# One engine for the low parts of the weights, and new durations in the planner that sets the order

## Chip, core and metric

One core of one Trainium2 chip. The metric is the device time of one execution in microseconds, the median of several runs. The profile is one execution taken by the hardware profiler.

## What is computed

Two layers over 256 tokens of width 1024 (cut to what matters):

```python
for l in range(DEPTH):                       # DEPTH = 2
    proj = x @ w_in[l]                       # split into the branches' inputs and the gates
    ya = rg_lru(conv(pa_x), ...) * gelu(pa_g)               # branch A
    yb = rms(gated_delta_rule(q, k, v, g, beta)) * silu(z)  # branch B
    yc = rms(gla(q, k, v, log_a)) * silu(r)                 # branch C
    merged = sum(sigmoid(gate_i) * (y_i @ w_branch[l, i]) for y_i in (ya, yb, yc))
    x = layer_norm(alpha * x + merged @ w_out[l])
    x = layer_norm(alpha * x + (silu(x @ w1[l]) * (x @ w3[l])) @ w2[l])
```

All in float32. Branch B solves, for each chunk of tokens and each head, a unit triangular system; the kernel does this by inverting 8x8 blocks first and joining them step by step.

## The kernel before

**Weights.** All weight matrices of a layer are cut into 146 units of 128x1024 float32 in the order in which TensorE uses them (`ORDER`, `NU`). SyncE's queue loads each unit into one of four `raw` tiles (`load_w`). `split_w` then makes two tiles of it in a rounded format that TensorE takes at full rate: ScalarE copies `raw` to `hi`, and the low part `lo = raw - hi` is a tensor_tensor of 128x1024 elements. Each matmul of the reference becomes three: x_hi with hi, x_lo with hi, x_hi with lo. Most `lo` are made by VectorE (line 304); of the units with an even number from 8 to 58 of each layer, 26 a layer, GpSimd makes them (line 432). These units belong to the first part of a layer, the projections and branches. `fill` keeps 6 split units ahead of TensorE (14 in the last branch). After each split the next unit's load is issued.

**Main work and chains.** `main` is a generator that emits TensorE's units in the order of `ORDER`: `tm` and `fm` (projections), `br`, `wo`, `f` and `w` (the feed-forward part). Everything that follows from a product (convolutions, activations, the triangular solve with its small matmuls `pk`, `pR`, `px`, `pp`, `pt`, the norms) sits in other generators, the chains, each with a priority. A chain yields at each point where it has to wait for something.

**The planner.** Each engine runs its instructions in the order in which they are emitted, so the emission order decides how a late result holds up an engine. `Order` works it out while the program is built: it keeps a clock for each engine, `op` adds a cost to it for each instruction (formulas in the helpers: `act_fn`, `dve`, `mm`, `tp` and so on), and `drive` emits a chain's next step when, by these clocks, its inputs were ready `SLACK` = 1.5 us before TensorE's clock (priority 0: no slack) and neither ScalarE's nor VectorE's clock is more than `LOAD` = 9 us ahead of TensorE's. Otherwise it emits the next piece of main work. Real waits are made by semaphores; a cost that is wrong moves an instruction in its engine's order, nothing else. A step put too early makes TensorE wait in place; one put too late delays its chain.

**Branch B's chain** (`b_inv`), as far as the text needs it: ScalarE scales the products `pk` into `At`; VectorE multiplies `At` with the decay `E`; a copy of 128x64 elements starts `z` (inside the tile `sub`); a product `pR` follows; then a loop of 14 small dependent VectorE instructions alternates between `pR` and `z`; one VectorE instruction spreads `z` into `Y`; and TensorE transposes `Y` (`px`). After it come the joining steps `pp`, `pt`, `px`. GpSimd also computes the inverse square roots (`rsqrt`: `rk`, `rq`, `ycf`, `ybf`, `rs`), of 8 columns or of one.

Of the kernel before, what the change touches and what calls it, by code (L numbers as in the profile page):

```python
# [8 lines left out]
F32 = mybir.dt.float32  # L9
# [6 lines left out]
MULT, ADD, SUB, MAX, MIN = ALU.mult, ALU.add, ALU.subtract, ALU.max, ALU.min  # L16
# [7 lines left out]
NF = FF // P  # L24
ALPHA = float((2.0 * L) ** 0.25)
RAW, AHEAD, FAR, SLACK, SLOTS = 4, 6, 14, 1.5, 37
PMOD, PLO, PHI = 2, 8, 60
LOAD = (99.0, 9.0, 9.0, 9.0, 9.0)
DKB = float(128 ** -0.5)
DKC = 0.125  # L30
# [42 lines left out]
NU = len(ORDER)  # L73
# [81 lines left out]
          AF.Silu: "u", AF.Gelu_apprx_tanh: "g"}  # L155


class Order:


# [12 lines left out]
    def op(self, eng, cost, ready=0.0):  # L173
        t = max([self.clk[eng], self.ready, ready] +
                [f for e, f in self.fin.items() if e != eng])
        t += cost
        self.clk[eng] = t
        self.fin[eng] = t
        return t

    def end(self):
# [68 lines left out]
def _build(ctx, nc, tc, ins, out):  # L250
    V, A, G, T = nc.vector, nc.scalar, nc.gpsimd, nc.tensor
    pool = lambda name, bufs, **k: ctx.enter_context(tc.tile_pool(name=name, bufs=bufs, **k))
# [6 lines left out]
    O = Order()  # L259
    def TOK(i):  # L260
        tc.stamp_issue_order_token(i.ins, "tbl")
    def PIN(i):
        if MODE == 2: TOK(i)
        else: tc.keep_in_program_order(i)
    def n_of(ap):
        n = 1
        for d in ap.shape[1:]:
            n *= d
        return n

    def slot(name, dt=F32):
        return t4.tile([P, 1024], dt, tag="t4k", name=name)
# [11 lines left out]
    def act_fn(o, i, f, **k):  # L284
        aps = sum(not isinstance(v, float) for v in k.values())
        sets = TABLES.get(f)
        if sets is not None and O.table not in sets:
            O.table = sets[0]
            O.op("act", 1.28)
            if f == AF.Exp:  # L290
                PIN(A.preload_act_table_set("natural_log_exp_and_others"))
        ins_ = A.activation(o, i, f, **k)  # L292
        if sets is not None and MODE:
            TOK(ins_)
        O.op("act", 0.12 + 0.09 * aps + 0.000833 * n_of(o))

    def cp(o, i):
        act_fn(o, i, AF.Copy)

    def dve(o, x=0.0):  # L300
        O.op("dve", 0.13 + x + 0.00104 * n_of(o))

    def tt(o, a, b, op):
        V.tensor_tensor(out=o, in0=a, in1=b, op=op)  # L304
        dve(o)
# [8 lines left out]
    def stt(o, a, s, b, op0, op1):  # L314
        V.scalar_tensor_tensor(out=o, in0=a, scalar=s, in1=b, op0=op0, op1=op1)  # L315
        dve(o, 0.06)
# [16 lines left out]

    def recip(o, i):
        V.reciprocal(o, i)
        dve(o, 0.0075 * n_of(o))

    def rsqrt(o, i, e):
        G.tensor_tensor(out=o, in0=i, in1=e, op=ALU.pow)  # L339
        O.op("pool", 0.3 + 0.17 * n_of(o))  # L340

    def split(hi, lo, src):
        cp(hi, src)
        tt(lo, src, hi.bitcast(F32), SUB)

    def mm(o, w, x, start=True, stop=True):
        T.matmul(o, w, x, start=start, stop=stop)  # L347
        n, m = n_of(x), n_of(w)
        if w.dtype == F32R:
            O.op("pe", max(n, m, 128) / 2400.0)  # L350
        else:
            O.op("pe", max(n, m, 32) / 600.0)

    def tp(o, i, idn):
        T.transpose(o, i, idn)  # L355
        O.op("pe", 0.107)

    def h4(t):
        return t.rearrange("p (h c) -> p h c", h=4)
# [37 lines left out]
    raws, ready, pos = [], [], [0, 0]  # L397

    def halves(i):
        n = 512 if i < 1 else 1024  # L400
        return [slice(c, c + n) for c in range(0, 1024, n)]

    def load_w(between=None):
        i = len(raws) + pos[1]
        if i >= L * NU:
            return
        l, j = divmod(i, NU)
        t = wraw.tile([P, 1024], F32, tag="raw", name="raw")
        for c in halves(i):
            nc.sync.dma_start(out=t[:, c], in_=ins["w"][l, j][:, c])  # L410
            if i == 0 and c.start == 0:
                between()
        O.clk["dma"] = max(O.clk["dma"], O.clk["pe"] - 4.0) + 1.5
        raws.append((t, O.clk["dma"] + 2.0))

    def split_w(between=None):
        if not raws:
            return
        t, at = raws.pop(0)
        i, j = pos[1], pos[1] % NU  # L420
        pos[1] += 1
        keep = O.ready, O.fin
        O.begin(at)
        hi, lo = slot("hi", F32R), slot("lo", F32R)
        for c in halves(i)[:-1]:
            split(hi[:, c], lo[:, c], t[:, c])
            between()
        c = halves(i)[-1]
        hi_, lo_, t_ = hi[:, c], lo[:, c], t[:, c]
        cp(hi_, t_)  # L430
        if j % PMOD == 0 and PLO <= j < PHI:
            G.tensor_tensor(out=lo, in0=t, in1=hi.bitcast(F32), op=SUB)  # L432
            O.op("pool", 2.4)
        else:
            tt(lo_, t_, hi_.bitcast(F32), SUB)
        ready.append((hi, lo, O.end()))
        O.ready, O.fin = keep
        load_w()
# [61 lines left out]
    def layer(l, xs, xtok):  # L500
# [5 lines left out]
        def done(n):  # L506
            O.done(k_(n))
# [527 lines left out]
        def ln_chain(tk, halves, lv, xs_out, is_out, name):  # L1035
            g, b = lv
            s = xr[:, tk]
            c = 512 if len(halves) == 2 else 256
            st = sml.tile([P, 4, 6], F32, tag="st", name="st")
            c0 = 0  # L1040
            for n, ps in enumerate(halves):
                sl = slice(c0, c0 + ps.shape[1])
                yield k_(f"{name}ps{tk}{n}")
                stt(s[:, sl], s[:, sl], ALPHA, ps, MULT, ADD)
                if tk and n:
                    yield
                for c0 in range(sl.start, sl.stop, c):
                    V.bn_stats(st[:, c0 // c], s[:, c0:c0 + c])
                    O.op("dve", 0.1 + 0.001 * c)
                c0 = sl.stop  # L1050
            mv, rs = sm("mv", [P, 2]), sm("rs", [P, 1])
            V.bn_aggr(mv, st[:, 0:D // c].rearrange("p a b -> p (a b)"))
            ts(rs, mv[:, 1:2], 1e-5, ADD)
            rsqrt(rs, rs, mhalf[:, 0:1])
            if is_out and tk:
                dst = out[tk * P:(tk + 1) * P]
                c, nb = slice(768, 1024), sm("nb", [P, 1])
                stt(nb, mv[:, 0:1], -1.0, rs, MULT, MULT)
                act_fn(s[:, c], s[:, c], AF.Identity, scale=rs, bias=nb)
                G.tensor_tensor(out=s[:, c], in0=s[:, c], in1=g[:, c], op=MULT)  # L1060
                G.tensor_tensor(out=s[:, c], in0=s[:, c], in1=b[:, c], op=ADD)
                A.dma_start(out=dst[:, c], in_=s[:, c])
                for c in (slice(0, 384), slice(384, 768)):
                    stt(s[:, c], s[:, c], mv[:, 0:1], g[:, c], SUB, MULT)
                    stt(s[:, c], s[:, c], rs, b[:, c], MULT, ADD)
                    nc.sync.dma_start(out=dst[:, c], in_=s[:, c])
                return
            h = [slice(0, 512), slice(512, 1024)]
            stt(s[:, h[0]], s[:, h[0]], mv[:, 0:1], g[:, h[0]], SUB, MULT)
            stt(s[:, h[0]], s[:, h[0]], rs, b[:, h[0]], MULT, ADD)  # L1070

            def second():
                stt(s[:, h[1]], s[:, h[1]], mv[:, 0:1], g[:, h[1]], SUB, MULT)
                stt(s[:, h[1]], s[:, h[1]], rs, b[:, h[1]], MULT, ADD)

            def fm(n, between):
                ps = h4(bank("pln"))
                for q in range(4):
                    c0 = 512 * n + 128 * q
                    tp(ps[:, q], s[:, c0:c0 + P], ident)  # L1080
                o = [[xs_out[i][2 * n + q][:, :, tk * P:(tk + 1) * P] for q in range(2)]
                     for i in range(2)]
                for q in range(2):
                    cp(o[0][q], ps[:, 2 * q:2 * q + 2])
                between()
                for q in range(2):
                    tt(o[1][q], ps[:, 2 * q:2 * q + 2], o[0][q].bitcast(F32), SUB)

            if is_out:
                nc.sync.dma_start(out=out[tk * P:(tk + 1) * P, h[0]], in_=s[:, h[0]])  # L1090
                second()
                nc.sync.dma_start(out=out[tk * P:(tk + 1) * P, h[1]], in_=s[:, h[1]])
                return
            yield
            fm(0, second)
            yield
            fm(1, lambda: None)
            done(f"{name}{tk}")
            if tk:
                ahead[0] = AHEAD  # L1100
# [250 lines left out]
    with tc.manual_schedule(engines={mybir.EngineType.SP}):  # L1351
# [9 lines left out]
        for q in range(4):  # L1361
            if q % 2 == 0:
                tp2 = pair2("xin")
            t = tp2[q % 2]
            n = 1 if q else 2
# [99 lines left out]
```

## Time and profile before

| | us |
|---|---|
| median of 3 runs | 942.83 (942.8, 942.83, 944.91) |
| profiled execution | 939.84 |
| its span, first to last instruction | 938.0 |

The profiled execution is 1.84 us longer than its span. Busy times in the profile are per engine; a matmul's end is modelled, and consecutive matmuls overlap, so that TensorE's rate is read from the starts of consecutive matmuls and not from their lengths. "PE" is TensorE, "DVE" VectorE, "ACT" ScalarE, "POOL" GpSimd, "SPq" SyncE's queue.

### The profile page before, as it was taken

The page shows a single profiled execution, that of the slowest core. Times are in us where ns is not written, and L with a number is a line of the kernel's source. Part 1 is how long each engine was busy: PE and PEld are TensorE (multiplying, and loading weights), DVE is VectorE, ACT ScalarE, POOL GpSimd, SP SyncE. Part 2 cuts the span into 40 slices and gives each one's busy share as a digit, 9 for nine tenths or more (in the row PEclk, how much of TensorE's full clock was granted, in tenths as well). Part 3 has the DMA queues.
Part 4 walks back from the last instruction along what each step waited for, and adds up shares of the span by engine and source line. Part 5 has one row for each costly group of instructions (what it writes and reads, how often), then busy time and mean ns, then how long its engine had stood idle before and what let it go on. Part 6 is the DMA issues. An engine that isn't in the chain of part 4 may idle for free.

```text
span 938.0 us, 15814 instructions
## 1 busy us (share of the span) xinstructions
PE 922.5 (98%) x6306; PEld 838.3 (89%) x6306; DVE 644.5 (69%) x965; ACT 523.6 (56%) x824; POOL 162.4 (17%) x81
## 2 busy tenths in 40 slices
PE   7999999999999999999999999999999999999996
PEld 5998899999988888888889998999999888888885
DVE  5577975695875776676457699586768648667715
ACT  5877669644733665555145774973547147566600
POOL 0454512530000000000033351253300000000001
PEclk9999999999999999999999999999999999999998
DMA  8854324546770865568325352255568338655801
GB/s 273 266 182 148 101 69 130 173 149 234 249 290 3 299 215 180 182 240 275 111 72 191 121 158 96 72 155 195 181 217 280 132 117 271 219 180 180 286 7 45
DMA packets 47994, 162.84 MB, mean 174 GB/s; under 512 B 7537, under 2 KB 8497, under 8 KB 47793
## 3 DMA queue, kind: packets, MB, share of 16 engines
q1 hardware_dynamic: 47776, 161.71, 51.6%
q8 instruction: 49, 0.80, 0.3%
q14 instruction: 25, 0.20, 0.1%
q10 hardware_dynamic: 144, 0.13, 0.0%
HBM read 160.77 MB, written 1.05 MB: 173 GB/s over the span
## 4 chain that ended last, share of the span: by engine, by line
PE 92%; DVE 5%; DMA 1%; issue 1%; ACT 1%; POOL 0%; SPq 0%; POOLq 0%
PE fm L347 26%; PE f L347 22%; PE w L347 13%; PE tm L347 11%; PE br L347 7%; PE wo L347 5%; PE pt L347 1%; PE pp L347 1%; DVE sub L304 1%; DMA raw<-in_w_dram 1%; DVE lo L304 1%; PE pr L347 1%; PE px L355 1%; PE pln L355 1%; DVE xa L315 1%
## 5 line engine op out<-in xcount | busy, mean ns | idle before, releaser
L304 DVE TENSOR_TENSOR lo<-raw,hi 128x1024 fp32r<-128x1024 f32 (+1 forms) x241 | 310.0, 1305 | 108.9 <-ACT hi L292 101.7
L292 ACT ACTIVATE hi<-raw 128x1024 fp32r<-128x1024 f32 (+1 forms) x293 | 300.8, 1053 | 86.0 <-DMA raw<-in_w_dram 75.8
L347 PE MATMUL fm<-x,hi 128*128 128x256 f32 x1536 | 283.4, 286 | 0.0
L347 PEld LDWEIGHTS fm<-x,hi 128*128 128x128 f32 x1536 | 239.8, 192 | 2.1 <-issue 1.8
L347 PE MATMUL fm<-x,lo 128*128 128x256 f32 x768 | 217.7, 283 | 0.0
L347 PE MATMUL f<-x,hi 128*128 128x512 f32 x576 | 202.0, 396 | 0.0
L432 POOL TENSOR_TENSOR lo<-raw,hi 128x1024 fp32r<-128x1024 f32 x52 | 134.4, 2587 | 230.9 <-ACT hi L292 225.6
L347 PE MATMUL f<-x,lo 128*128 128x256 f32 x576 | 160.7, 279 | 0.0
L347 PEld LDWEIGHTS fm<-x,lo 128*128 128x128 f32 x768 | 147.4, 192 | 0.0
L347 PEld LDWEIGHTS f<-x,hi 128*128 128x128 f32 x576 | 108.1, 188 | 26.1
L347 PE MATMUL w<-hi,hh 128*128 128x512 f32 (+1 forms) x396 | 111.2, 367 | 0.0
L347 PEld LDWEIGHTS f<-x,lo 128*128 128x128 f32 x576 | 108.5, 188 | 0.1
L347 PE MATMUL tm<-hi,x 128*128 128x512 f32 x320 | 101.3, 400 | 3.6 <-ACT hi L292 3.6
L339 POOL TENSOR_TENSOR rs<-rs,mhalf 128x1 f32<-128x1 f32 x8 | 7.5, 936 | 524.2 <-DVE rs L309 524.2
L347 PEld LDWEIGHTS w<-hi,hh 128*128 128x128 f32 x396 | 71.4, 189 | 12.2
L347 PEld LDWEIGHTS tm<-hi,x 128*128 128x128 f32 x320 | 59.5, 191 | 17.0 <-ACT hi L292 5.2
L347 PE MATMUL w<-lo,hh 128*128 128x512 f32 (+1 forms) x198 | 72.4, 366 | 0.0
L347 PE MATMUL tm<-lo,x 128*128 128x512 f32 x160 | 62.3, 392 | 0.0
L347 PEld LDWEIGHTS w<-lo,hh 128*128 128x128 f32 x198 | 37.3, 188 | 6.2
L292 ACT ACTIVATE x<-pln 128x256 fp32r<-128x256 f32 x24 | 7.9, 383 | 60.7 <-PE pln L355 60.7
L347 PE MATMUL wo<-hi,mh 128*128 128x512 f32 x128 | 39.8, 392 | 0.0
L292 ACT ACTIVATE gt<-fm,vecs 128x256 f32<-128x256 f32 x48 | 20.3, 468 | 33.7 <-PE fm L347 33.6
(277 smaller groups left out, 1151.7 us busy)
## 6 DMA issues: line engine op xcount, KB each, us to landing
raw<-in_w_dram SPq DMA_DIRECT2D x291, 512.0 KB, 4.4
lnv<-in_lnv_dram SPq DMA_DIRECT2D x8, 512.0 KB, 7.4
xr<-in_xtm_dram SPq DMA_DIRECT2D x1, 1024.0 KB, 7.5
xin<-in_xfm_dram SPq DMA_DIRECT2D x3, 256.0 KB, 7.6
raw<-in_w_dram SPq DMA_DIRECT2D x2, 256.0 KB, 3.5
ar<-in_aw_dram SPq DMA_DIRECT2D x8, 64.0 KB, 4.2
out_dram<-xr SPq DMA_DIRECT2D x2, 256.0 KB, 2.1
kc<-in_kc_dram SPq DMA_DIRECT2D x1, 476.0 KB, 9.3
```

Of the source, the lines that this page charges most:

```text
L292: ins_ = A.activation(o, i, f, **k)
L304: V.tensor_tensor(out=o, in0=a, in1=b, op=op)
L315: V.scalar_tensor_tensor(out=o, in0=a, scalar=s, in1=b, op0=op0, op1=op1)
L339: G.tensor_tensor(out=o, in0=i, in1=e, op=ALU.pow)
L347: T.matmul(o, w, x, start=start, stop=stop)
L355: T.transpose(o, i, idn)
L432: G.tensor_tensor(out=lo, in0=t, in1=hi.bitcast(F32), op=SUB)
```

## The change

Two things. All `lo` are made by VectorE: the constants `PMOD, PLO, PHI` and the branch in `split_w` that gave 26 units a layer to GpSimd go. And the planner's durations are replaced; a result now reaches another engine `LAT` later than its own engine is free again. `SLACK`, `LOAD`, the number of tiles and the work itself stay.

```diff
-PMOD, PLO, PHI = 2, 8, 60
+LAT = {"pe": 0.17, "act": 0.12, "dve": 0.1, "pool": 0.1}
...
         t += cost
         self.clk[eng] = t
-        self.fin[eng] = t
+        self.fin[eng] = t + LAT.get(eng, 0.0)
...
-        O.op("act", 0.12 + 0.09 * aps + 0.000833 * n_of(o))
+        O.op("act", 0.09 + 0.09 * aps + 0.000833 * n_of(o))
...
     def dve(o, x=0.0):
-        O.op("dve", 0.13 + x + 0.00104 * n_of(o))
+        O.op("dve", 0.055 + x + 0.00104 * n_of(o))
...
-        dve(o, 0.0075 * n_of(o))
+        dve(o, 0.006 * n_of(o))
...
-        O.op("pool", 0.3 + 0.17 * n_of(o))
+        O.op("pool", 0.85 + 0.1 * n_of(o))
...
         if w.dtype == F32R:
-            O.op("pe", max(n, m, 128) / 2400.0)
+            O.op("pe", max(n, 2 * m) / 2400.0 + 0.0135)
         else:
-            O.op("pe", max(n, m, 32) / 600.0)
+            O.op("pe", max(n, m, 32) / 600.0 + 0.011)
...
-        O.op("pe", 0.107)
+        O.op("pe", 0.109)
...
-        O.clk["dma"] = max(O.clk["dma"], O.clk["pe"] - 4.0) + 1.5
+        O.clk["dma"] = max(O.clk["dma"], O.clk["pe"] - 4.0) + 1.85
...
         cp(hi_, t_)
-        if j % PMOD == 0 and PLO <= j < PHI:
-            G.tensor_tensor(out=lo, in0=t, in1=hi.bitcast(F32), op=SUB)
-            O.op("pool", 2.4)
-        else:
-            tt(lo_, t_, hi_.bitcast(F32), SUB)
+        tt(lo_, t_, hi_.bitcast(F32), SUB)
...
-                    O.op("dve", 0.1 + 0.001 * c)
+                    O.op("dve", 0.07 + 0.00104 * c)
```

## Rows read from the trace of the kernel before

**Rows 1.** The page's busy time of each engine over the span.

```profile
PE 922.5 (98%) x6306; PEld 838.3 (89%) x6306; DVE 644.5 (69%) x965; ACT 523.6 (56%) x824; POOL 162.4 (17%) x81
```

**Rows 2.** Windows: length, busy time (instructions) of each engine, granted clock, DMA.

```profile
26.00:210.00 184.00, 181.73 (x1551) 176.01 (x1551) 138.22 (x230) 128.15 (x208) 77.29 (x34) 0.99 0.48 151
100.00:121.00 21.00, 18.73 (x141) 18.08 (x141) 20.48 (x42) 11.37 (x21) 10.47 (x5) 0.92 0.34 101
545.00:590.00 45.00, 44.45 (x353) 42.05 (x353) 39.71 (x79) 28.18 (x52) 15.08 (x7) 1.00 0.35 115
```

**Rows 3.** Timeline of TensorE near 117 us: start, us, instruction, idle before and releaser.

```profile
117.51 1.94 PE L355 MATMUL px<-kc,Y 128*128 128x128 f32 x8 [2.27 <-DVE Y L304]
```

**Rows 4.** Timeline of VectorE, 98 to 117 us.

```profile
98.42 0.69 DVE L304 TENSOR_TENSOR At<-At,E 128x512 f32<-128x512 f32 x1
...
100.89 2.38 DVE L319 COPY sub<-kc 128x64 f32<-128x64 f32 x1
...
107.47 2.42 DVE L315 SCALAR_TENSOR_TENSOR xa<-fm,vecs,xa 128x255 f32<-128x255 f32 x6
...
109.93 1.52 DVE L309 TENSOR_SCALAR rq<-rq 128x8 f32<-128x8 f32 x1
...
112.78 2.05 DVE L304 TENSOR_TENSOR sub<-sub 128x32 f32<-128x32 f32 x1
...
116.13 1.23 DVE L304 TENSOR_TENSOR Y<-sub,kc 128x1024 f32<-128x1024 f32 x1
```

**Rows 5.** Timeline of GpSimd in the same stretch.

```profile
97.93 2.07 POOL L339 TENSOR_TENSOR ycf<-ycm,mhalf 128x8 f32<-128x8 f32 x1 [4.76 <-DVE ycm L311]
100.12 3.09 POOL L432 TENSOR_TENSOR lo<-raw,hi 128x1024 fp32r<-128x1024 f32 x1
...
112.36 2.42 POOL L432 TENSOR_TENSOR lo<-raw,hi 128x1024 fp32r<-128x1024 f32 x1 [0.94 <-ACT hi L292]
```

**Rows 6.** Chain that ended last, 545 to 600 us: start, us, engine and line.

```profile
548.35 1.89 DVE ssk L309
...
556.87 2.32 DVE sub L319
...
560.90 2.71 issue
...
567.82 0.22 DVE sub L304
...
584.99 0.66 PE px L355 x4
...
587.70 1.79 PE pp L347 x16
...
593.80 2.88 PE fm L347 x24
```

**Rows 7.** Groups of TensorE instructions, 545 to 590 us: count, busy us, mean ns.

```profile
L347 PE MATMUL fm<-x,hi 128*128 128x256 f32 x128 | 24.1, 288 | 0.0
L347 PE MATMUL fm<-x,lo 128*128 128x256 f32 x63 | 18.0, 285 | 0.0
...
L347 PE MATMUL tm<-hi,x 128*128 128x512 f32 x8 | 2.6, 410 | 0.0
...
L347 PE MATMUL pR<-sub,kc 128*128 128x512 f32 x2 | 1.1, 630 | 0.0
```

**Rows 8.** Low parts on VectorE: 300 to 450, 30 to 210, 484 to 668 us.

```profile
L304 DVE TENSOR_TENSOR lo<-raw,hi 128x1024 fp32r<-128x1024 f32 x64 | 76.7, 1220 | 21.9 <-ACT hi L292 18.2 <-PE w L347 3.5
L304 DVE TENSOR_TENSOR lo<-raw,hi 128x1024 fp32r<-128x1024 f32 x27 | 42.0, 1562 | 16.5 <-ACT hi L292 16.5
L304 DVE TENSOR_TENSOR lo<-raw,hi 128x1024 fp32r<-128x1024 f32 x26 | 43.9, 1690 | 15.2 <-ACT hi L292 12.6 <-issue 2.6
```

**Rows 9.** The page's group of low parts on GpSimd, whole span.

```profile
L432 POOL TENSOR_TENSOR lo<-raw,hi 128x1024 fp32r<-128x1024 f32 x52 | 134.4, 2587 | 230.9 <-ACT hi L292 225.6
```

**Rows 10.** Waits of SyncE's queue: us in total, times, longest.

```profile
SPq L410 <- POOL lo L432: 172.3, 43, 14.6
```

More of the change, by code (lines that the diff above doesn't have):

```diff
@@ L419, in split_w @@
         t, at = raws.pop(0)
-        i, j = pos[1], pos[1] % NU
+        i = pos[1]
         pos[1] += 1
```

## The prediction

> **What bounds the kernel now.** I read the page's busy times first, then windows, then TensorE's waits and the timelines around them. TensorE is busy 98% of the span [rows 1]. Its rate is that of its own pitch: 24 `fm` matmuls take 2.88 us on the chain that ended last, 0.120 us each, 16 of 128 columns 1.79 us, 0.112 each [rows 6]. Nothing in the change alters the number or shape of a matmul, so only time in which TensorE does not keep this pitch can be won. The windows show where that is. Over most of the span the chain that ended last stays on TensorE; it leaves it for long in two places, both where branch B's chain meets VectorE at its limit: 100 to 121 us (first layer), with VectorE busy 20.48 of 21, and 545 to 590 us (second), with 39.71 of 45 [rows 2]. The reader is to see VectorE nearly full in both, at 75% (138.22 of 184) over the whole first part of a layer.
>
> First place: `px` waits 2.27 us for `Y` [rows 3]. The granted clock of the stretch is 0.92 [rows 2]; after that idle time TensorE ran at the lower of its two levels, 1.2 GHz, for a while, which is (1 - 0.92) x 21 = 1.7 us. Together 4.0 us.
>
> Second place: no long wait, but the chain that ended last runs over VectorE from `ssk` to `px` at 584.99 [rows 6]. TensorE's loss there I count: 191 `fm` matmuls [rows 7] x 0.120 = 22.9 us; the other 162 of the 353 [rows 2], in 13 more groups, at 0.112 = 18.1; together 41.0 of 45, so at most 4.0 is lost. The 512-wide `tm` (8 with `hi` shown, and one with `lo` for each two) and the two `pR` need two to four times that price [rows 7], which adds about 2. From below, 0.55 us is plainly idle (45 - 44.45) [rows 2]. I take 2.0. The two places hold 6.0 us, 0.64% of the time. The start (waiting for the first weights; the first 8 units never used GpSimd) and the last norm are untouched.
>
> **The low parts.** 52 instructions leave GpSimd, 2587 ns each, 134.4 us [rows 9]; GpSimd keeps about 28 of 162.4 us. VectorE gets 52 more at 1220 ns, the mean of a stretch without GpSimd [rows 8]: 52 x 1.22 = 63.4 us, 32 a layer. If nothing came back, 26 to 210 us would hold 138 + 32 = 170 of 184 us, 92%.
>
> But much comes back. In the stretches with GpSimd's low parts VectorE's own `lo` take 1562 and 1690 ns in place of 1220 [rows 8]: 27 x 0.34 + 26 x 0.47 = 21.4 us. Single instructions are stretched more: a 128x64 copy takes 2.38 us, a 128x8 `rq` 1.52, a 128x32 `sub` 2.05 [rows 4], where a dependent small one takes 0.22 [rows 6]. The copy ends at 103.27, GpSimd's `lo` at 103.21; `sub` at 114.83, `lo` at 114.78 [rows 4, 5]: each ended as GpSimd's instruction ended. So the delay goes with GpSimd's low parts. In the first place it is 2.2 + 1.3 + 1.8 = 5.3 us, all ahead of `Y`. Three low parts ran on GpSimd from 100 to 115 us (of five instructions there, two are `ycf` and `rq`'s root); on VectorE they cost 3 x 1.22 = 3.7. Net `Y` is 1.6 us earlier if all three come ahead of it and 5.3 if none does, against a wait of 2.27. In the second place 1.7 (`ssk`) + 2.1 (copy) + 2.1 (the "issue" of 2.71, the rest of a 128x512 tensor_tensor that takes 0.69 elsewhere) [rows 4, 6] = 5.9 come back and four low parts cost 4.9 (seven GpSimd instructions in the window [rows 2], three of them roots): net 1.0. VectorE's busy time over the span then is 644.5 + 63.4 - 21.4 - 11.2 = 675 us at most, 72%.
>
> The Trainium skill, SBUF — State Buffer, section "Who interferes with whom", gives the rule: a VectorE instruction with two SBUF inputs, or in a two-port mode, is blocked for the whole of a GpSimd instruction that reads SBUF. The trace agrees for the low parts. It does not for GpSimd's roots: `At`, two inputs in SBUF, took 0.69 us at 98.42 inside `ycf`'s 2.07 us [rows 4, 5]. By the rule the roots that stay would go on blocking; by the rows nothing is left that does.
>
> The loads: SyncE's queue waited 172.3 us in 43 waits for GpSimd's low parts to free a `raw` tile [rows 10]. These now end on VectorE, each 2587 - 1220 = 1.4 us shorter but queued behind VectorE's other work. The DMA share is 0.48 and 0.35 in the two windows [rows 2], so a load that goes out a few us late is hidden by the 6 units (17 us of `fm` pitch) kept ahead; without that cover each late unit would stop TensorE and VectorE's queue would be the price. The planned load time (1.5 to 1.85) moves splits in the plan, not the order of loads. I count nothing.
>
> **The planner's durations.** A unit's 24 matmuls cost 24 x 256/2400 = 2.56 us before and 24 x 0.1202 = 2.88 now; the row says 2.88 [rows 6]. TensorE's planned clock ran 11% fast, so steps were planned with more matmuls ahead of them than they needed; that reserve goes. A 128x512 tensor_tensor costs 0.055 + 0.532 = 0.587 in its own queue and 0.687 to another engine; the row says 0.69 [rows 4]. Six independent `xa` start in 2.42 us [rows 4], about 0.40 each; planned 0.38. For small dependent ones it is wrong: the loop before `Y` has 14, at 56 to 8 elements, planned 14 x 0.055 + 448 x 0.00104 = 1.24 us; the chain shows 0.22 for one [rows 6], 3.1 in all. The planner puts `px` 1.9 us too early, of which `SLACK` covers 1.5. Old formula: 2.29, 0.8 too early, within `SLACK`; what broke it was the 5.3 us that no cost held. I charge 0.4 us a layer for this.
>
> **Sum.** First place: 4.0 - 0.4 = 3.6, the low clock gone with the wait. Second: VectorE stays nearly full (39.7 - 1.0 of 45), so I take half of 2.0 as left and 0.4 of the rest: 0.6 won. Together 4.2. Profiled execution: 939.84 - 4.2 = 935.6. The median of runs is 2.99 us above the profiled one: 942.83 - 4.2 = 938.6. A measurement of this kernel can tell 0.3%, 2.8 us, from no change: the bounds are 940.0 and 945.7.
>
> **The rivals.** *The waits move* (within 0.3%). Each queue gets another order, with less reserve in it, so `px`, `pp` and `pt` meet late results by tenths of a microsecond in both layers, and one wait as long as 2.27 us brings the low clock again. For it: VectorE's 20.48 of 21. Against it: the delays that made the wait are no longer there. It needs 1.4 of the 4.2 us lost again; I set 941.5.
>
> *VectorE becomes the bound* (slower). If the long VectorE instructions have another cause than GpSimd, the low parts are added to two stretches that are already full: 3.7 and 4.9 us on the chain that TensorE waits for, 942.8 + 8.6 = 951.4. It decides where an added `lo` finds no idle VectorE. Against it: the ends that coincide [rows 4, 5] and 1220 ns where GpSimd is still.
>
> *The planner underprices all of VectorE* (slower). The fixed cost falls by 0.075 us an instruction. If none of that time were saved in the queue, 79 instructions in the second place would run 5.9 us ahead of the truth and 42 in the first 3.2 [rows 2]; less 1.5 of `SLACK` each that is 6.1 us of waits, with 1.7 for the clock, on top of the forecast: 946.4. It decides when instructions follow each other at their full length. Against it: `xa`, six in 2.42 us. The Trainium skill, VectorE: DVE Perf Modes, section "The DRAIN you can't avoid", says that the next instruction does not start until the pipeline is empty; that speaks for this rival and against the new 0.055. The trace has both: the small dependent ones wait out, the `xa` do not.
>
> *Nothing is won because TensorE is at its floor* is the forecast's own limit: 6.0 us at most.
>
> **Chances.** Forecast (936.5 to 940.0) 0.56; the waits move (940.0 to 945.7) 0.24; VectorE the bound 0.08; underpriced 0.07; another unplanned wait, on a tile or a PSUM bank, that the new order meets, 0.05. Faster: 0.56 plus 0.04 of the last two, 0.60; same 0.24; slower 0.16. For 8 in 10 the range goes from 935.5 (all 6.0 won, and 1 for short waits elsewhere) to 945.5, leaving out VectorE as the bound and most of the underpriced case. The likeliest case alone is 936.5 to 940.0.
>
> **What would show it.** Right: GpSimd with 29 instructions and under 30 us; all `lo` near 1220 ns; the copy, `rq` and `sub` near 0.2; VectorE under 675 us with 1017 instructions; no wait of `px` over 0.5 us and no window under 0.99 in the clock after the start. Wrong: `lo` still at 1500 and more, a group of TensorE waits for `lo`, or a new wait over 2 us with a clock window under 0.95.

## The result and the profile after

The change makes the kernel slower by 0.7%: 949.21 us median (948.46 to 949.56) against 942.82 of the kernel before on the same chip, ratio 1.007, 95% interval 1.0054 to 1.0086. I had forecast 938.6. The profiled execution took 949.44 us with a span of 947.7.

The page's busy times, which answer to [rows 1]:

```profile
PE 925.6 (98%) x6306; PEld 841.3 (89%) x6306; DVE 642.4 (68%) x1017; ACT 525.9 (55%) x826; POOL 26.7 (3%) x29
```

VectorE executes 52 instructions more and is busy 2.1 us less. Its group of low parts over the span has a mean of 1222 ns; the stretch without GpSimd's low parts had 1220 [rows 8]:

```profile
L307 DVE TENSOR_TENSOR lo<-raw,hi 128x1024 fp32r<-128x1024 f32 x291 | 349.9, 1222 | 112.4 <-ACT hi L295 107.0 <-PE w L350 3.4
```

So the first half of the change did what it says and cost VectorE no busy time. The time is lost elsewhere. Windows, in the columns of [rows 2], of the first part of layer 1 and of the two places:

```profile
26.00:210.00 184.00, 178.67 (x1517) 172.09 (x1516) 138.66 (x254) 126.52 (x205) 7.94 (x6) 0.98 0.47 150
95.00:120.00 25.00, 19.67 (x143) 18.33 (x142) 21.71 (x53) 13.71 (x23) 2.01 (x1) 0.86 0.39 125
560.00:595.00 35.00, 30.77 (x244) 29.93 (x244) 30.73 (x68) 25.54 (x47) 3.06 (x2) 0.95 0.34 108
```

and TensorE's waits over the span (us in total, times, longest):

```profile
PE px L358 <- DVE Y L307: 4.7, 1, 4.7
...
PE pt L350 <- ACT pb L295: 2.4, 1, 2.4
PE pR L350 <- DVE sub L307: 1.8, 1, 1.8
```

The two places are the same as before, and both got worse. First: `px` waits 4.7 us in place of 2.27 [rows 3]. The granted clock of 0.86 over the window of 25 us would be (1 - 0.86) x 25 = 3.5 us, but it falls while TensorE still waits, where it costs nothing more; after the wait it costs (1 - 0.55) x 4.6 = 2.1 us:

```profile
109.40:114.00 4.60, 4.60 (x24) 4.60 (x25) 3.75 (x7) 3.08 (x6) 0.00 (x0) 0.55 0.22 61
```

That is 6.8 us in place of 4.0. Second: 1.8 + 2.4 us of waits and (1 - 0.95) x 35 = 1.75 of clock, 6.0 in place of the 2.0 estimated. Together 6.8 us more. The two medians differ by 6.4 us and the two profiled executions by 9.6.

What stands between the product and the transposes shows on TensorE's timeline and in its groups from 99.7 to 109.3 us:

```profile
98.74 1.02 PE L350 MATMUL pR<-sub,kc 128*128 128x512 f32 x2
99.78 0.30 PE L358 MATMUL pyf<-kc,ycy 128*128 128x128 f32 x1
100.72 1.11 PE L358 MATMUL pyf<-kc,ycy 128*128 128x128 f32 x7 [0.64 <-DVE ycy L318]
...
109.38 1.94 PE L358 MATMUL px<-kc,Y 128*128 128x128 f32 x8 [4.67 <-DVE Y L307]
```

```profile
L350 PE MATMUL fm<-x,hi 128*128 128x256 f32 x16 | 3.0, 288 | 0.0
L350 PE MATMUL fm<-x,lo 128*128 128x256 f32 x8 | 2.3, 282 | 0.0
L358 PE MATMUL pyf<-kc,ycy 128*128 128x128 f32 x8 | 1.4, 298 | 0.7 <-DVE ycy L318 0.6
...
```

24 `fm` matmuls and 8 transposes, 3.8 us of work. The kernel before had three units there (groups of before, 106 to 115.4 us), 72 x 0.120 = 8.6 us:

```profile
L347 PE MATMUL fm<-x,hi 128*128 128x256 f32 x48 | 9.1, 291 | 0.0
L347 PE MATMUL fm<-x,lo 128*128 128x256 f32 x24 | 6.8, 283 | 0.0
```

VectorE meanwhile (timeline after, columns of [rows 4]):

```profile
90.99 0.69 DVE L307 TENSOR_TENSOR At<-At,E 128x512 f32<-128x512 f32 x1 [1.07 <-ACT At L295]
...
95.26 0.18 DVE L322 COPY sub<-kc 128x64 f32<-128x64 f32 x1
...
99.29 2.15 DVE L318 SCALAR_TENSOR_TENSOR ycy<-co,ycf,sr 128x128 f32<-128x128 f32 x8
101.36 1.21 DVE L307 TENSOR_TENSOR lo<-raw,hi 128x1024 fp32r<-128x1024 f32 x1
102.49 2.42 DVE L318 SCALAR_TENSOR_TENSOR q<-fm,vecs,q 128x255 f32<-128x255 f32 x6
104.83 0.21 DVE L307 TENSOR_TENSOR sub<-pR,sub 128x56 f32<-128x56 f32 x1
...
107.80 0.17 DVE L307 TENSOR_TENSOR sub<-sub 128x8 f32<-128x8 f32 x1
108.00 1.22 DVE L307 TENSOR_TENSOR Y<-sub,kc 128x1024 f32<-128x1024 f32 x1
```

None of these is stretched any more: the copy takes 0.18 us (2.38 before). But after `pR` come 5.5 us of other work in VectorE's queue (`ycy`, `lo`, `q`) and then the loop, 3.2 us, and `Y`. From the end of `pR` to the end of `Y` that is 9.5 us, with 3.8 us of matmuls to cover it.

In the second place the chain that ended last reads:

```profile
579.53 2.35 DVE xa L318 x6
...
581.96 0.63 ACT xah L295
582.59 0.50 ACT pb L295
...
583.13 2.50 PE pt L350 x16
```

`pt` waits for `pb` on ScalarE, `pb` stands in ScalarE's queue behind `xah` of another branch, and `xah` waits for `xa` on VectorE: an order again. VectorE is busy throughout these lines, so they do not rule out its load; `lo_only` and `plan_only` below speak against it.

### The profile page after: what moved, and what is told of

It reads as the page before. It is cut to its first block, busy times and chain, and to the rows that moved or that the text cites. A ratio compares the mean times of both kernels' runs of the same rounds, so it can differ in the third digit from the quotient of the medians.

```text
span 947.7 us, 15772 instructions
## 1 busy us (share of the span) xinstructions
PE 925.6 (98%) x6306; PEld 841.3 (89%) x6306; DVE 642.4 (68%) x1017; ACT 525.9 (55%) x826; POOL 26.7 (3%) x29
## 4 chain that ended last, share of the span: by engine, by line
PE 90%; DVE 5%; ACT 2%; issue 1%; DMA 1%; POOL 0%; SPq 0%; POOLq 0%; ACTq 0%; DVEq 0%
PE fm L350 26%; PE f L350 21%; PE w L350 13%; PE tm L350 10%; PE br L350 7%; PE wo L350 5%; DVE lo L307 1%; PE pt L350 1%; PE pp L350 1%; DVE sub L307 1%; DMA raw<-in_w_dram 1%; PE pr L350 1%; DVE q L318 1%; PE pln L358 1%; PE px L358 1%
## 5 line engine op out<-in xcount | busy, mean ns | idle before, releaser
L307 DVE TENSOR_TENSOR lo<-raw,hi 128x1024 fp32r<-128x1024 f32 (+1 forms) x293 | 351.3, 1218 | 114.1 <-ACT hi L295 108.7
L350 PEld LDWEIGHTS tm<-lo,x 128*128 128x128 f32 x160 | 30.5, 190 | 6.7 <-DVE lo L307 0.2
L307 DVE TENSOR_TENSOR hv<-f,hv 128x256 f32<-128x256 f32 x36 | 15.2, 422 | 29.9 <-ACT hv L295 29.9
```

## The experiments

Each kernel was run beside the kernel before on the same chip; the ratio is to that. Theories: A, the new order leaves TensorE too little work between a result and the step that needs it; B, the added low parts load VectorE; C, the order is thin because the plan counts time in which TensorE waits; and, from pe_free on, D, a chain that comes later runs short of matmuls at its end.

| kernel | median us | ratio, 95% interval |
|---|---|---|
| the change | 949.21 | 1.007 (1.0054 to 1.0086) |
| lo_only | 941.9 | 0.9997 (0.9983 to 1.0012) |
| plan_only | 953.09 | 1.0123 (1.0101 to 1.0144) |
| pyf_first | 945.81 | 1.0048 (1.0032 to 1.0065) |
| zprice | 950.57 | 1.0098 (1.0078 to 1.0118) |
| pe_free | 939.2 | 0.997 (0.9954 to 0.9986) |
| pe_free_z | 944.69 | 1.0027 (1.0017 to 1.0037) |
| slack3 | 937.52 | 0.9948 (0.9932 to 0.9964) |
| slack3_z | 936.79 | 0.9938 (0.9924 to 0.9953) |
| plan_slack3 | 943.3 | 1.0017 (1.0006 to 1.0027) |
| lo_slack3 | 946.44 | 1.0051 (1.0037 to 1.0065) |
| dve13 | 950.27 | 1.0087 (1.0073 to 1.0101) |
| slack45_z | 943.74 | 1.0023 (1.001 to 1.0036) |

### The two halves apart

**lo_only**: the kernel before with

```diff
-        if j % PMOD == 0 and PLO <= j < PHI:
-            G.tensor_tensor(out=lo, in0=t, in1=hi.bitcast(F32), op=SUB)
-            O.op("pool", 2.4)
-        else:
-            tt(lo_, t_, hi_.bitcast(F32), SUB)
+        tt(lo_, t_, hi_.bitcast(F32), SUB)
```

> The kernel before with one edit: VectorE makes all low parts; the planner's old durations stay. Theory A (the order: the new plan leaves TensorE too few matmuls between the product pR and the transposes px, while VectorE is still in the 14-step loop between them): no loss, and the delays by GpSimd gone, so 938 to 943, px waiting under 1 us in the first layer. Theory B (load: the 52 added low parts themselves make VectorE late): 947 to 951, with px waits like those of the changed kernel (4.7 us).

941.9 us, no change. Its windows (first and second place, and a new one), and the largest of TensorE's waits after the start:

```profile
95.00:125.00 30.00, 30.00 (x252) 29.52 (x251) 29.45 (x69) 19.29 (x35) 4.65 (x2) 1.00 0.35 107
545.00:595.00 50.00, 50.00 (x422) 49.21 (x422) 41.42 (x87) 30.30 (x50) 5.35 (x3) 1.00 0.43 137
603.00:620.00 17.00, 14.13 (x97) 13.63 (x96) 8.58 (x11) 16.86 (x28) 0.00 (x0) 0.80 0.31 93
```

```profile
PE pt L346 <- ACT pb L291: 2.9, 2, 1.8
```

With VectorE full (29.45 of 30 us) and all low parts on it, TensorE is busy throughout both old places, with the clock at 1.00: the forecast for the low parts, and B falls. But in the second layer the order now puts `pb` behind ScalarE's work for branch A (ScalarE is busy 16.86 of the 17 us), and 2.9 us of waits and at most 0.20 x 17 = 3.4 us of clock go there. What the low parts gave back, an order that nobody chose for it took away.

**plan_only**: the changed kernel with those lines put back.

> The changed kernel with the low parts given back to GpSimd as before; the planner's new durations stay. Theory A (order): as slow as the changed kernel or slower, 947 to 953, since the thin stretches stay and GpSimd's delays come back. Theory B (load): back to 941 to 944.

953.09 us, just past the upper end of A's range (953); B's 941 to 944 is far off. The waits are at `pR` and `px`, and the low parts are slow again (30 to 210 us):

```profile
PE pR L351 <- DVE sub L308: 5.7, 2, 4.4
...
PE px L359 <- DVE Y L308: 3.8, 2, 2.1
```

```profile
L308 DVE TENSOR_TENSOR lo<-raw,hi 128x1024 fp32r<-128x1024 f32 x26 | 39.9, 1533 | 21.2 <-ACT hi L296 20.7 <-issue 0.2
```

The new durations alone cost more than the whole loss.

### Why the new order is thin

Following the planner's own clocks through the changed kernel, `Y` is done at 113.98 us and `px` is emitted when TensorE's planned clock is past that by `SLACK`. Between `pR` and `px` this clock moves by 3.76 us of matmuls and by 3.85 us of waiting: the second half of the `pyf` transposes is charged a wait for the evacuation of the first half, because `op` lets each instruction of a step wait for all earlier ones of the step on other engines. On the chip the second half goes to another bank and waits for nothing of the kind: seven of the eight transposes run in one piece at 100.72 us. The plan of the kernel before, followed in the same way, lets TensorE wait 5.9 us at this `pyf` step, but behind `px` and not ahead of it.

**pyf_first**: the changed kernel with

```diff
+            pys = []
             for t in range(2):
                 ps = bank("pyf").rearrange("p (t k c) -> p t k c", t=2, k=2)
                 ...
-                ps = ps.rearrange("p t k c -> p t (k c)")
+                pys.append(ps.rearrange("p t k c -> p t (k c)"))
+            for ps in pys:
                 a, b = pair2(name + "h", F32R)
```

> The changed kernel with one edit: in the norm of a branch the 8 transposes pyf are emitted before the two evacuations, where before each half's evacuation followed its four transposes. Same work. Theory C (a part of A: the planner's TensorE clock is advanced by 3.85 us inside this step, time in which the plan lets TensorE wait for an evacuation and the chip does not, and in the first layer this falls between pR and px, so that px follows pR after 32 matmuls and 8 transposes): one more unit of 24 matmuls, 2.9 us, gets between pR and px, px waits 1.8 us and not 4.7, and 945 to 947. Theory B, and A with its cause in the loop's price alone: 948 to 950, px still waits over 4 us.

945.81 us. (The count there should be 24 matmuls and 8 transposes, as the rows above show.) The wait of 4.7 us is gone altogether, where 1.8 was expected to stay, and the clock of the first place is at 1.00. Waits are left in the first layer (1.3 us at a joining step, 1.0 at `pt`) and in the second (2.9 at a joining step, 1.8 at `pR`):

```profile
PE px L358 <- DVE Y L326: 4.2, 2, 2.9
...
PE pR L350 <- DVE sub L307: 1.8, 1, 1.8
```

```profile
95.00:120.00 25.00, 22.43 (x180) 20.86 (x179) 24.09 (x57) 16.37 (x29) 0.22 (x1) 1.00 0.41 145
```

The plan puts one unit more ahead of `px`, 48 `fm` in place of 24. The trace has 65 (groups, 98.9 to 109.8 us; all stand ahead of `px`):

```profile
L350 PE MATMUL fm<-x,hi 128*128 128x256 f32 x44 | 8.0, 285 | 0.0
L350 PE MATMUL fm<-x,lo 128*128 128x256 f32 x21 | 5.9, 283 | 0.0
```

So the order that TensorE runs is not in every place the one in which the planner emits, though the description of the planner says so, and 17 of the 41 added matmuls are not the plan's doing. What moved them is not shown.

**zprice**: the changed kernel with the loop's true price.

```diff
                 tt(z[:, :, k + 1:], z[:, :, k + 1:], tmp[:, :, k + 1:], ADD)
+            O.op("dve", 1.86)
```

> The changed kernel with the loop of 14 small VectorE instructions priced 1.86 us higher in the planner, which is what the trace shows. Nothing else. Theory A with its cause in the loop's price: px moves behind more matmuls in both layers and the time falls by 2 us or more, under 947.2. Theory C: in the first layer the added price only lengthens the plan's wait inside the pyf step, px stays where it is and waits 4 to 5 us; 947 to 950, with any gain in the second layer alone.

950.57 us. The wait after `Y` is the same 4.7 us to the tenth, and in the second layer the 2.4 us at `pt` have given place to 2.9 at a joining step:

```profile
PE px L358 <- DVE Y L307: 4.7, 1, 4.7
...
PE px L358 <- DVE Y L326: 2.9, 1, 2.9
```

The better price went into the planned wait (3.85 to 5.71 us), not into matmuls. C holds for the first place.

**dve13**: the rival of the prediction, VectorE underpriced.

```diff
-        O.op("dve", 0.055 + x + 0.00104 * n_of(o))
+        O.op("dve", 0.13 + x + 0.00104 * n_of(o))
```

> The changed kernel with VectorE's fixed cost in the planner back at 0.13 us, SLACK 1.5. The rival of the prediction (0.055 underprices all VectorE instructions, and that made the order too early): 938 to 943. Theory C: the higher price turns into plan time in which TensorE waits (7.1 us between pR and px in both layers, with 4.6 us of matmuls), so no better than the changed kernel: 946 to 952.

950.27 us; the rival falls. TensorE waits 6.7 us for the joining steps' `Y` and 1.9 for the first:

```profile
PE px L358 <- DVE Y L326: 6.7, 4, 2.3
...
PE px L358 <- DVE Y L307: 1.9, 2, 1.2
```

### A right clock, or more reserve

**pe_free** and **pe_free_z**: the changed kernel, and zprice, with

```diff
-                [f for e, f in self.fin.items() if e != eng])
+                [f for e, f in self.fin.items() if e != eng and eng != "pe"])
```

> The changed kernel with one edit in the planner: a TensorE instruction of a chain's step no longer waits, in the plan, for the other engines' instructions of the same step (it still waits for what the step as a whole needs). Theory C (plan time in which TensorE waits inside a step and the chip does not is what makes the order thin): the plan has 6.6 us of matmuls between pR and px in both layers in place of 3.8 and 5.8, px waits under 1 us, 938 to 944. Theory D (the branch's chain of dependent steps is as long as the matmuls that can hide it, so a wait taken away at px comes back at a later step): 946 to 951, with the sum of TensorE's waits unchanged.

> The last kernel (TensorE's waits inside a step taken out of the plan), and the loop of 14 small VectorE instructions priced 1.86 us higher as the trace shows. Theory C: 9.5 us of matmuls between pR and px, no wait there, and no low clock after the start: 937 to 941. By the loop's price alone, without C, this edit by itself was worth nothing (950.6), so a gain over the last kernel would show that the price counts once the plan's TensorE clock is right. Theory D: 946 to 951.

939.2 us, in C's range and 0.3% faster than before, and 944.69, a miss. In neither does TensorE wait in the two places. In pe_free 48 `fm` and 8 transposes stand between `pR` (105.01 us) and `px` (112.49) of the first layer, as the plan has it. But D has a part in both: with matmuls in place of planned waits each step of the chain comes later, and the last ones (`pp`, `pw`, `pS`) run when few matmuls are left to cover them. Windows of that stretch in pe_free, then in pe_free_z:

```profile
165.00:185.00 20.00, 18.50 (x173) 17.52 (x172) 6.64 (x16) 5.62 (x9) 0.94 (x2) 0.74 0.23 66
```

```profile
620.00:645.00 25.00, 21.28 (x209) 19.54 (x208) 12.88 (x26) 10.68 (x19) 0.00 (x0) 0.73 0.14 47
```

The clock alone costs up to 0.26 x 20 = 5.2 and 0.27 x 25 = 6.8 us there (less by what falls in waits).

**slack3** and **slack3_z**: the changed kernel, and zprice, with

```diff
-RAW, AHEAD, FAR, SLACK, SLOTS = 4, 6, 14, 1.5, 37
+RAW, AHEAD, FAR, SLACK, SLOTS = 4, 6, 14, 3.0, 37
```

> The changed kernel with SLACK at 3.0 us in place of 1.5, nothing else. Theory A (too little reserve between a result and the TensorE step that needs it): 6.6 us of matmuls between pR and px in both layers, 942 to 946. Theory D: 947 to 951.

> The changed kernel with SLACK at 3.0 us and the loop priced 1.86 us higher. Theory A: 9.5 us of matmuls between pR and px in both layers, no wait at px, 939 to 944. Theory D: 947 to 951, TensorE's waits moved to the joining steps pp and pt.

937.52 and 936.79 us: both beat the kernel before, by 0.5 and 0.6%, and better than A expected. In slack3_z TensorE is busy in every microsecond of both places (windows), and past the start its longest waits sum to 1.4 us:

```profile
95.00:120.00 25.00, 25.00 (x209) 24.47 (x208) 23.16 (x54) 15.55 (x27) 4.58 (x2) 1.00 0.39 123
560.00:595.00 35.00, 35.00 (x298) 34.47 (x297) 30.15 (x68) 21.41 (x39) 5.76 (x2) 1.00 0.34 103
```

```profile
PE pS L350 <- ACT w L295: 1.4, 2, 0.7
```

It is not more matmuls alone. In the first layer of slack3_z `ycy`, `lo` and `q` no longer stand between `pR` (104.55 us) and the loop, VectorE waits for `pR`, and `Y` is done 4.5 us after its end, where the change needed 9.5:

```profile
105.61 0.22 DVE L307 TENSOR_TENSOR sub<-pR,sub 128x56 f32<-128x56 f32 x1 [1.36 <-PE pR L350]
...
108.80 1.23 DVE L307 TENSOR_TENSOR Y<-sub,kc 128x1024 f32<-128x1024 f32 x1
```

How much of the gain is the matmuls and how much VectorE's order was not separated. The price of the loop, worth nothing alone, is not shown to be worth anything here either: the two intervals overlap.

**plan_slack3**: slack3 with the low parts back on GpSimd.

> The changed kernel with SLACK at 3.0 us and the low parts given back to GpSimd. As with SLACK 3.0 and VectorE's low parts (937.5) the plan has 6.6 us of matmuls between pR and px in both layers, so the two differ in who makes the low parts. If GpSimd's delays of VectorE cost TensorE time under a good order too: 941 to 947, with waits at pR or px and VectorE's single instructions stretched to 1.5 us and more. If a good order hides them: 936 to 939.

943.3 us, 0.7% over slack3. The plan is equally wide at `px`; the waits that are left are at `pt` (5.3 us in all), behind VectorE instructions that GpSimd stretches (chain that ended last; `xah` takes 0.68 us elsewhere):

```profile
119.70 2.19 DVE xah L308
121.89 2.35 DVE v L319 x6
...
124.38 1.69 PE pt L351 x13
```

So moving the low parts is worth some 6 us once the order lets it through.

**lo_slack3**: lo_only with `SLACK` at 3.0.

> The kernel before with the low parts on VectorE and SLACK at 3.0 us; the planner's old durations. Theory C: in the first layer this plan has 4.3 us of matmuls between pR and px and lets TensorE wait 10.6 us there, which the chip does not, so px waits again: 942 to 948. If a longer SLACK is all that counts, whatever the durations: 935 to 939.

946.44 us, in the range of C; the wait is one step before the one I named, at `pR`:

```profile
PE pR L346 <- DVE sub L303: 2.4, 1, 2.4
```

A longer `SLACK` by itself, with the old durations, makes things worse (0.9997 to 1.0051).

**slack45_z**: zprice with `SLACK` at 4.5.

> The changed kernel with SLACK at 4.5 us and the loop priced 1.86 us higher. If more reserve in the plan is more reserve on the chip: 934 to 937, at least as fast as with 3.0. Theory C: of the 13.1 us between pR and px in this plan 6.6 are TensorE waiting, 6.6 are matmuls, less than the 9.5 with SLACK 3.0: 937 to 943.

943.74 us, a little above C's range. More slack is not faster, as C said, but not for C's reason: `px` does not wait, and 72 `fm` and 8 transposes stand ahead of it on the trace (115.4 to 125.3 us), more than the 6.6 us of the plan. The chain starts 10 us later (`pR` at 115 us, 104.6 in slack3_z) and its joining steps run short of cover, as in pe_free_z:

```profile
PE pp L350 <- DVE Y L322: 2.7, 3, 1.2
```

```profile
620.00:645.00 25.00, 23.67 (x254) 23.19 (x253) 13.37 (x23) 12.69 (x23) 0.00 (x0) 0.86 0.32 101
```

## Why the prediction was wrong

**What bounds the kernel: right.** Only lost pitch of TensorE could be won, and it was lost in those two places. slack3_z, which empties both, gains 0.6%, against 6.0 us, 0.64%, estimated. (The two profiled executions, 939.84 and 936.81 us, differ by 3.0 only.)

**The low parts: right, and better than said.** GpSimd keeps 29 instructions and 26.7 us; the `lo` take 1222 ns on average; the copy takes 0.18. VectorE's busy time went to 642.4 us, not to 675 at most: 33 us more came back, which I put down to single stretched instructions that I did not list. lo_only shows both places free. The roots that stay on GpSimd do not stretch VectorE's instructions: `At`, two inputs in SBUF, took 0.69 us at 90.99 while this one ran, and the two others of this kind that ran beside a root (`At` in the second layer, `xah`) 0.69 and 0.68:

```profile
89.94 1.65 POOL L342 TENSOR_TENSOR ycf<-ycm,mhalf 128x8 f32<-128x8 f32 x1 [1.08 <-DVE cS L307]
```

By the Trainium skill, SBUF — State Buffer, section "Who interferes with whom", the two contend for an exclusive lock on a shared port pair; this pair shows no delay, and the measurement decides.

**The planner's durations: the step that failed.** I checked the new costs against rows one instruction at a time, found them right but for the loop, and charged 0.4 us a layer for that. But an order is not made of single costs. TensorE's planned clock also moves when the planner lets it wait, and that I did not follow. In place of 0.4 us the first layer lost 4.7 us at `px` and 2.1 us of clock, and the second 4.2 and 1.75. pyf_first, which removes one such planned wait and no work, takes the first loss away, with 17 matmuls beyond what its plan gave; pe_free, which removes them all and has at `px` what its plan gave, takes both away; zprice, which mends the cost that I blamed, does not touch the first. The kernel before was no better built, only lucky at `px` (72 matmuls): its own planned wait of 5.9 us fell behind `px`, and lo_only, with the old durations, meets a new late result in another place.

**The sum** took both losses as won: 3.6 and 0.6 us. They went to -2.8 and -4.0.

**The rivals.** "The waits move" was the right kind, at 0.24, but priced at less than what there was to win; the waits grew past the old ones. VectorE as the bound: shown wrong by lo_only. "The planner underprices all of VectorE" came near in time (946.4) by a wrong mechanism: dve13 puts the price back and stays at 1.0087. The rule of the Trainium skill that the next VectorE instruction does not start until the pipeline is empty (VectorE: DVE Perf Modes, "The DRAIN you can't avoid") spoke for it; a plan priced nearer to that rule did not win the time back. What I left out is a rival in which costs that are nearer the truth make a worse order.

Open: why the second layer's order fails at `pR` and `pt` was not separated; pe_free and slack3 remove those waits along with the rest. At `pR` it is not a lack of matmuls: 87 `fm` run from 557.3 to 569.4 us, between the products `pk` and `pR`, and the chain that ended last lies mostly on VectorE from 545 to 574 us, where `lo`, `q` and `catt` stand among the steps that lead to `pR`. There VectorE comes late, and whether planned waits made it so is not shown.

## What to carry to other kernels

When an order is planned from durations, read what lies between a result and the step that needs it in real matmuls, not in the planner's clock, and look for time that the plan spends waiting and the chip does not. Costs nearer the truth can take away a reserve that wrong costs gave by accident; change the reserve with them, and test it on both sides, since a chain that starts too late runs out of cover at its end. A gain that is real in the engine that got it (no stretched instructions in lo_only) is not seen in the time until the order lets it through (slack3 against plan_slack3).

## What the runs showed of the hardware

The granted clock cost the changed kernel 2.1 + 1.75 us beside 8.9 us of waits. After the one wait of 4.7 us it was 0.55 over 4.6 us, most of them at the lower of its two levels (1.2 GHz); in pe_free_z, where none of the waits at the end of the chain exceeds 1.6 us, it was 0.73 over 25 us, with `pw`, `pS` and `pkS` one behind the other. In slack3_z the two waits of 0.7 us at `pS` left the clock at 1.00 in the windows around them (160 to 175 and 620 to 640 us). GpSimd's 128x1024 low part stretched VectorE instructions of 8 to 512 columns to 1.5 to 2.9 us each, which is more in total than VectorE needs to do the 52 itself: it took over 52 x 1.222 = 63.5 us of work and was busy 2.1 us less, so some 65 us of stretching went.
